# The second layer's modulation vectors made beside the first expert stage: a two-part network on one core

## The chip, the cores and the metric

The kernel runs on one core of a Trainium2 chip. The metric is the device time of one execution, in microseconds (us); lower is better. The core's engines are TensorE (PE, with its weight loads as PEld), VectorE (DVE), ScalarE (ACT), GpSimd (POOL) and SyncE (SP, which here only issues transfers). Each engine runs its own list of instructions in a fixed order and waits on semaphores; a transfer is queued by the engine that issues it.

## The reference, cut to what matters

Two networks of two layers each run one after the other on 1024 tokens of width 1024. The first is an S5 layer and an attention layer. The second has an even layer (window attention, a gating unit) and an odd layer (latent attention, a short convolution), each followed by a stage of 16 experts in which every expert takes the 128 tokens that it scores highest. The even layer also updates 256 context tokens, the odd layer does not.

Every layer is modulated: from one conditioning vector `c` come vectors that scale, shift and gate its activations.

```
silu_c, silu_cc = silu(c), silu(c_ctx)
for layer in range(2):
    m_lat = split(silu_c  @ mod_w[layer] + mod_b[layer], 6)      # six vectors of 1024
    m_ctx = split(silu_cc @ mod_w[layer] + mod_b[layer], 6)
    h = rms_norm(x, g1) * (1 + m_lat[1]) + m_lat[0]
    x = x + m_lat[2] * mixer(h)                                  # even or odd
    h = rms_norm(x, g2) * (1 + m_lat[4]) + m_lat[3]
    x = x + m_lat[5] * experts(h)
    ... the same for the context, in the even layer alone
return rms_norm(x, final_g)
```

The weights `mod_w[layer]` are 1024 by 6144 numbers of fp32. The vectors depend on `c` and weights only, so they may be made at any time before their use.

## The kernel before, in words

All products are fp32, made of three fp32r products each: a matrix is split into a high and a low part (`whi` on ACT, `wlo` on DVE, L282 and L283 for the expert weights, L241 and L242 for others), and `mm3` issues the three matmuls (L247 to L249).

**The modulation.** `mod_steps` makes one of the vectors ("a part", 1024 numbers) in eight steps of 128 columns. A step does the product of the weights with `silu(c)` on POOL, not on TensorE: in two halves, SP loads 512 by 128 weights (`mraw`, 256 KB, L364, two buffers), POOL multiplies them by the vector (L367), adds the halves of the result (L373), and gathers what is left into `macc` (L378 in the first half, L375 and L376 in the second). What remains is a sum over the 128 partitions, which PE does as a matmul of `macc` with a column of ones (L396, called "the sum" below); DVE adds the bias (L399) into a column or into `mrow`. After the eighth step `mrow` is transposed on PE and stored.

A step's sum isn't issued in the step itself but at the start of the next one, by `rest()`; a ninth entry of the list issues the last. Where the result goes in PSUM is `mod_psum`'s choice: one bank of its own (`pC`), or, while `self.attending` is set, one of three banks (`pT`) that the transposes use.

**When a step runs.** The list `self.behind` holds the steps of all parts in the order of their use, each with a weight (2 where the context's vector is made too, else 1). The loops of the layers call `tick()` after each group of products; a tick takes from the list as much weight as `self.rate[1]` says. `require(key)` runs at once all that is left up to a part that is about to be needed. So modulation runs beside the layers, from the S5 layer on. During the expert stages (`ffn`) the rate is (0, 0), so that none runs there. When the first expert stage begins, some 30 steps of weight 1 are still in the list (the rest of the second layer's first gate, then its scale, shift and gate around the experts); they run beside the odd layer.

**Who sets the order.** The code is traced once and a list scheduler, driven by a simulated timeline, puts the instructions of each engine in order: an instruction stands where its operands are ready in that timeline and its turn in the program has come. The chip then keeps to that order.

**The expert stage.** Per expert, POOL gathers 128 tokens (`xs`, L2253, one buffer), PE transposes them (L2202), and three products with 1024 by 1024 weights follow: w1 (`first`), w3 (`second`), w2 (`third`). SP loads the weights as 24 tiles of 512 KB (`exp_w`, L2172) into a ring of some 21 buffers; each is split by ACT and DVE into one of five buffers. After the 48 matmuls of a product, 16 short ones (L2241, into `pC`) do the context's tokens with the unsplit tiles, and only then is a tile's buffer free. POOL adds the results to memory (`x_d`, L2298, `c_d`, L2302).

After the 16th expert the odd layer begins: its weights (`wraw`, from `od_w_in`) and the tokens (`xin`, from `x_d`) are loaded by SP, the tokens are normalised (ACT L291, DVE L224, POOL `rstd` L226, DVE L305), transposed (PE L312) and modulated (L313, L314).

Of the kernel before, what the change touches and what calls it, by code (L numbers as in the profile page):

```python
# [9 lines left out]
F32 = mybir.dt.float32  # L10
# [10 lines left out]
P = 128  # L21
# [101 lines left out]
class Net:  # L123
# [223 lines left out]
    def mod_steps(self, W, vecs, part, use):  # L347


        nc = self.nc  # L350
        G = nc.gpsimd.tensor_tensor
        todo = []

        def rest():
            while todo:
                todo.pop(0)()

        def step(q):
            rest()
            c0 = part * D + q * P  # L360
            acc = self.mp.tile([P, 2, P], F32, name="macc", bufs=3)
            for h in range(2):
                raw = self.mp.tile([P, 4, P], F32, name="mraw", bufs=2)
                nc.sync.dma_start(raw, W[h * 512:(h + 1) * 512, c0:c0 + P].rearrange("(k p) c -> p k c", p=P))  # L364
                for i, v in enumerate(vecs):
                    t = self.mp.tile([P, 4, P], F32, name="mprod")
                    mul = G(t, raw, v[:, 4 * h:4 * h + 4, None].to_broadcast([P, 4, P]), OP.mult)  # L367
                    if self.hold is not None:

                        self.tc.add_manual_dep(mul.ins, self.hold.ins.name, mybir.DependencyInfo(  # L370
                            mybir.DependencyClass.Sync, mybir.DependencyReason.DATA), reason="hold")
                        self.hold = None
                    G(t[:, 0:2], t[:, 0:2], t[:, 2:4], OP.add)  # L373
                    if h:
                        G(acc[:, i], acc[:, i], t[:, 0], OP.add)  # L375
                        G(acc[:, i], acc[:, i], t[:, 1], OP.add)  # L376
                    else:
                        G(acc[:, i], t[:, 0], t[:, 1], OP.add)  # L378
            todo.append(lambda: use(q, [[acc[:, i]] for i in range(len(vecs))], self.ones))

        return [lambda q=q: step(q) for q in range(KT)] + [rest]

    def mod_psum(self):
# [1719 lines left out]
    def ffn(self, layer, m, x_d, c_d, out=None):  # L2103
# [4 lines left out]
        with ExitStack() as ctx:  # L2108
# [87 lines left out]
            def matT(rows, xt):  # L2196

                for b in range(2):
                    ps = self.psT.tile([P, 512], F32, name="pT")
                    for j in range(4):  # L2200
                        k = 4 * b + j
                        nc.tensor.transpose(ps[:, j * P:(j + 1) * P], rows[:, k * P:(k + 1) * P], self.id)  # L2202
                    sl = slice(4 * b, 4 * b + 4)
                    self.split(xt[0][:, sl].rearrange("p k s -> p (k s)"), xt[1][:, sl].rearrange("p k s -> p (k s)"), ps)

            def matTc(rows, xc):

                ps = self.psT.tile([P, 512], F32, name="pT")
                n = 2 * CCAP
                for k in range(4):  # L2210
                    nc.tensor.transpose(ps[:, k * n:(k + 1) * n], rows[:, k * P:(k + 1) * P], self.id[:n, :n])
                nc.scalar.activation(xc.rearrange("p (h k) s -> p k h s", h=2),
                                     ps[:, :4 * n].rearrange("p (k h s) -> p k h s", k=4, h=2), AF.Copy)
# [3 lines left out]
            def product(W, xt, xc, hook=None):  # L2217


                with ExitStack() as order:  # L2220
                    if chain:
                        order.enter_context(self.tc.issue_after(chain[-1]))
                    ps = self.psA.tile([P, 2, 512], F32, name="pA")
                    pc = self.psC.tile([P, 512], F32, name="pC") if xc is not None else None
                    raws = []
                    for k in range(KT):
                        raw, hi, lo = wtile(W, k)
                        raws.append(raw)
                        if hook is not None:
                            hook(k)  # L2230
                        for n in range(2):
                            c = slice(n * 512, (n + 1) * 512)
                            last = self.mm3(ps[:, n], xt[0][:, k], xt[1][:, k], hi[:, c], lo[:, c], k == 0, k == KT - 1)
                cs = None
                if xc is not None:

                    with self.tc.issue_after(last.ins):
                        for k in range(KT):
                            for n in range(2):
                                t = 32 * (2 * (k % 2) + n)  # L2240
                                last = nc.tensor.matmul(pc[t:t + 32], lhsT=xc[:, k], rhs=raws[k][:, n * 512:(n + 1) * 512],  # L2241
                                                        start=(k < 2), stop=(k >= KT - 2))
                    chain.append(last.ins)
                    cs = ep.tile([2 * CCAP, 512], F32, name="cs", bufs=2)
                    nc.scalar.activation(cs, pc[64:128], AF.Copy)
                    nc.vector.tensor_tensor(cs, pc[0:64], cs, OP.add)
                return ps.rearrange("p a b -> p (a b)"), cs
# [3 lines left out]
            def fetch(e):  # L2251
                xs = ep.tile([P, D], F32, name="xs", bufs=1)
                nc.gpsimd.indirect_dma_start(out=xs, out_offset=None, in_=h_d,  # L2253
                                             in_offset=bass.IndirectOffsetOnAxis(ap=idx[:, e:e + 1], axis=0))
                xts[e] = [ep.tile([P, KT, P], F32R, name=f"xt{i}", bufs=2) for i in range(2)]
                matT(xs, xts[e])
                xcs[e] = None
                if c_d is not None:
                    xsc = ep.tile([2 * CCAP, 512], F32, name="xsc", bufs=1)
                    nc.gpsimd.indirect_dma_start(out=xsc, out_offset=None, in_=half_rows(hc_d),  # L2260
                                                 in_offset=bass.IndirectOffsetOnAxis(ap=idxc[:, e:e + 1], axis=0))
                    xcs[e] = ep.tile([P, KT, CCAP], F32, name="xc", bufs=2)
                    matTc(xsc, xcs[e])

            def first(e):
                pa, ca = product(a["exp_w1_2"][layer, e], xts[e], xcs[e])
                gs[e] = ep.tile([P, D], F32, name="g", bufs=1)
                nc.scalar.activation(gs[e], pa, AF.Silu)
                if ca is not None:
                    cgs[e] = ep.tile([2 * CCAP, 512], F32, name="cg", bufs=1)  # L2270
                    nc.scalar.activation(cgs[e], ca, AF.Silu)

            def second(e):
                pb, cb = product(a["exp_w3_2"][layer, e], xts[e], xcs[e])
                nc.vector.tensor_tensor(gs[e], pb, gs[e], OP.mult)
                gts[e] = [ep.tile([P, KT, P], F32R, name=f"gt{i}", bufs=1) for i in range(2)]
                matT(gs[e], gts[e])
                gcs[e] = None
                if cb is not None:
                    nc.vector.tensor_tensor(cgs[e], cb, cgs[e], OP.mult)  # L2280
                    gcs[e] = ep.tile([P, KT, CCAP], F32, name="gc", bufs=1)
                    matTc(cgs[e], gcs[e])
# [42 lines left out]
                final_norm(r)  # L2325
                nc.sync.dma_start(out[t * P:(t + 1) * P], r)

            self.rate = (0, 0)

            fetch(0)  # L2330
            first(0)
            for e in range(NEXP):
                if e + 1 < NEXP:
                    fetch(e + 1)
                second(e)
                if e + 1 < NEXP:
                    first(e + 1)
                third(e)
                self.tick()

# [71 lines left out]
```

## Time and profile before

| | |
|---|---|
| time, median of 3 runs | 4264.09 us (4262.44 to 4264.76) |
| the profiled execution: time, span | 4259.37 us, 4257.6 us |
| PE busy | 3920.6 us, 92% of the span |
| DVE busy | 2777.5 us, 65% |
| ACT busy | 1972.0 us, 46% |
| POOL busy | 1552.8 us, 36% |
| mean granted clock of PE | 0.962 of full speed |
| modulation multiplies on POOL (L367) | 416, of 1.13 us in the mean |

The stages by time in the span: S5 tables until about 340 us, the S5 layer and the attention's projections until about 1090, attention and the even layer until about 2060, the first expert stage to 2836, the odd layer to about 3640, the second expert stage to the end. Busy shares are means over stages with different limits, so the views of single stretches decide.

### The profile page before, as it was taken

The numbers are of one execution on the slowest core, as the hardware profiler recorded it, in microseconds if no ns is written. First come the engines' busy times: TensorE is split into PE (matmuls) and PEld (weight loads), VectorE is DVE, ScalarE is ACT, GpSimd is POOL, SyncE is SP. The second block draws the span as 40 slices with busy tenths as digits, with TensorE's granted clock in tenths as the row PEclk, the third lists the DMA queues.
The fourth block names the chain that finished last, engine by engine and source line by source line (L and its number), as shares of the span: only waits on it lengthen the run. The fifth ranks groups of instructions, "written<-read, shape, count | busy, mean of one in ns | idle before, by whom it ended". The sixth has DMA issues, their size and how long they took to land.

```text
span 4257.6 us, 58517 instructions
## 1 busy us (share of the span) xinstructions
PE 3920.6 (92%) x21173; PEld 2974.9 (70%) x21173; DVE 2777.5 (65%) x3962; ACT 1972.0 (46%) x3029; POOL 1552.8 (36%) x1723
## 2 busy tenths in 40 slices
PE   7888889999999999999799999979989999799997
PEld 6777667777566888568466666658876667588775
DVE  8695555352556635664777777764546654899887
ACT  4323232321554312542466666652245542577775
POOL 1005889998646788002211111126800002111003
PEclk9999999999999999999799999989999999899999
DMA  7536565345663553234688787862451025899996
GB/s 239 167 138 216 184 206 176 128 134 181 152 142 99 191 150 123 72 131 163 230 292 294 285 291 282 284 223 87 125 158 34 26 99 211 298 387 382 373 374 249
DMA packets 512339, 848.91 MB, mean 199 GB/s; under 512 B 68061, under 2 KB 300626, under 8 KB 511474
## 3 DMA queue, kind: packets, MB, share of 16 engines
q1 hardware_dynamic: 498946, 802.16, 55.1%
q0 software_dynamic: 13104, 43.01, 4.1%
q8 instruction: 167, 2.74, 0.3%
q14 instruction: 122, 1.00, 0.1%
HBM read 714.82 MB, written 130.21 MB: 198 GB/s over the span
## 4 chain that ended last, share of the span: by engine, by line
PE 63%; POOL 13%; DVE 11%; DMA 6%; issue 4%; ACT 2%; SPq 1%; POOLq 0%; ACTq 0%; DVEq 0%
PE pA L247 14%; PE pA L248 14%; PE pA L249 14%; POOL mprod L367 5%; PE pC L1059 4%; PE pC L2241 4%; PE pT L1075 4%; POOL mprod L373 4%; DVE S L968 2%; DVE sc L967 2%; DVE wlo L283 2%; POOL macc L376 1%; POOL macc L378 1%; POOL macc L375 1%; PE pT L2202 1%
## 5 line engine op out<-in xcount | busy, mean ns | idle before, releaser
L283 DVE TENSOR_TENSOR wlo<-fraw,whi 128x1024 fp32r<-128x1024 f32 x650 | 788.9, 1239 | 128.7 <-ACT whi L282 122.0
L282 ACT ACTIVATE whi<-fraw 128x1024 fp32r<-128x1024 f32 x650 | 679.9, 1060 | 195.8 <-PE pA L249 182.2
L247 PE MATMUL pA<-whi,ah 128*128 128x512 f32 (+3 forms) x1584 | 592.6, 375 | 6.1 <-ACT ah L282 4.1
L248 PE MATMUL pA<-wlo,ah 128*128 128x512 f32 (+3 forms) x1584 | 591.4, 373 | 3.1 <-DVE wlo L242 3.1
L249 PE MATMUL pA<-whi,al 128*128 128x512 f32 (+3 forms) x1584 | 589.5, 372 | 0.0
L248 PE MATMUL pA<-wlo,xt 128*128 128x512 f32 x1024 | 411.6, 402 | 4.3 <-POOL wlo L2182 2.1
L247 PE MATMUL pA<-whi,xt 128*128 128x512 f32 x1024 | 409.9, 401 | 1.8 <-ACT xt L282 1.8
L249 PE MATMUL pA<-whi,xt 128*128 128x512 f32 x1024 | 406.0, 397 | 0.6 <-DVE xt L283 0.6
L367 POOL TENSOR_TENSOR mprod<-mraw,sil 128x512 f32<-128x512 f32 x320 | 362.4, 1132 | 95.1 <-DMA mraw<-mod_w 71.8
L373 POOL TENSOR_TENSOR mprod<-mprod 128x256 f32<-128x256 f32 x416 | 349.5, 840 | 31.2
L2253 POOL DMA_INDIRECT xs<-h_d,ixl x32 | 38.7, 1210 | 834.3 <-PE pT L2202 809.6
L247 PEld LDWEIGHTS pA<-whi,ah 128*128 128x128 f32 x1584 | 302.5, 191 | 54.3 <-ACT ah L282 4.2
L248 PEld LDWEIGHTS pA<-wlo,ah 128*128 128x128 f32 x1584 | 302.2, 191 | 52.1 <-DVE wlo L242 4.9
L249 PEld LDWEIGHTS pA<-whi,al 128*128 128x128 f32 x1584 | 301.9, 191 | 48.3 <-issue 1.2
L241 ACT ACTIVATE whi<-wraw 128x1024 fp32r<-128x1024 f32 (+3 forms) x130 | 131.0, 1017 | 409.8 <-PE pA L249 185.8
L1028 DVE TENSOR_REDUCE st<-pA 128x1 f32<-128x640 f32 (+4 forms) x208 | 200.5, 967 | 137.8 <-PE pA L1348 62.7
L242 DVE TENSOR_TENSOR wlo<-wraw,whi 128x1024 fp32r<-128x1024 f32 (+3 forms) x130 | 174.0, 1356 | 123.4 <-ACT whi L241 121.7
L249 PE MATMUL pA<-ah,wlo 128*128 128x512 f32 x576 | 230.8, 403 | 12.9 <-DVE wlo L242 12.9
L247 PEld LDWEIGHTS pA<-whi,xt 128*128 128x128 f32 x1024 | 193.0, 188 | 61.8 <-issue 13.4
L247 PE MATMUL pA<-ah,whi 128*128 128x512 f32 x576 | 230.9, 404 | 3.6 <-ACT ah L282 2.4
L248 PE MATMUL pA<-al,whi 128*128 128x512 f32 x576 | 231.9, 403 | 1.0 <-DVE al L283 0.9
L248 PEld LDWEIGHTS pA<-wlo,xt 128*128 128x128 f32 x1024 | 193.2, 189 | 52.9 <-DVE wlo L283 7.8
(569 smaller groups left out, 8279.0 us busy)
## 6 DMA issues: line engine op xcount, KB each, us to landing
fraw<-exp_w SPq DMA_DIRECT2D x665, 512.0 KB
wraw<-exp_w SPq DMA_DIRECT2D x99, 512.0 KB
mraw<-mod_w SPq DMA_DIRECT2D x192, 256.0 KB
mraw<-b_mod_w SPq DMA_DIRECT2D x48, 256.0 KB
wraw<-a_w_in SPq DMA_DIRECT2D x16, 512.0 KB
mraw<-kv_mod_w SPq DMA_DIRECT2D x32, 256.0 KB
wraw<-kv_w SPq DMA_DIRECT2D x16, 512.0 KB
kf_d<-hs SPq DMA_DIRECT2D x32, 256.0 KB
```

The costliest lines, as they stand in the source:

```text
L242: nc.vector.tensor_tensor(lo[:, :kk, :n], raw[:, :kk, :n], hi[:, :kk, :n].bitcast(F32), OP.subtract)
L247: mm(ps, lhsT=lh, rhs=rh, start=first, stop=False)
L248: mm(ps, lhsT=lh, rhs=rl, start=False, stop=False)
L249: return mm(ps, lhsT=ll, rhs=rh, start=False, stop=last)
L282: self.nc.scalar.activation(hi, src, AF.Copy)
L283: self.nc.vector.tensor_tensor(lo, src, hi.bitcast(F32), OP.subtract)
L367: mul = G(t, raw, v[:, 4 * h:4 * h + 4, None].to_broadcast([P, 4, P]), OP.mult)
L373: G(t[:, 0:2], t[:, 0:2], t[:, 2:4], OP.add)
L1028: nc.vector.tensor_reduce(st[:, i:i + 1], s, AX.X, OP.max, negate=True)
L1059: mm = nc.tensor.matmul(box["acc"][s * 64:(s + 1) * 64, c], lhsT=v(kt, s), rhs=pt[s][:, c], start=(kt == 0), stop=(kt == last))
L1075: nc.tensor.transpose(pt[:, j * P:(j + 1) * P], ps_[s][j](kt), self.id)
L2241: last = nc.tensor.matmul(pc[t:t + 32], lhsT=xc[:, k], rhs=raws[k][:, n * 512:(n + 1) * 512], start=(k < 2), stop=(k >= KT - 2))
```

## The change

Two things are changed. In `mod_steps`, a step's sum is issued two steps later than before (`rest(2)` leaves two in the list), and `macc` has four buffers for three. In `ffn`, the rate during the expert loop is (0, 3) for (0, 0), `attending` is set, so that sums there go to the banks `pT`, and each expert ticks twice: after `second` and, as before, after `third`. For the second expert stage the list is empty.

```diff
-        def rest():
-            while todo:
+        def rest(keep=0):
+            while len(todo) > keep:
                 todo.pop(0)()
 
         def step(q):
-            rest()
+
+            rest(2)
             c0 = part * D + q * P
-            acc = self.mp.tile([P, 2, P], F32, name="macc", bufs=3)
+            acc = self.mp.tile([P, 2, P], F32, name="macc", bufs=4)
...
-            self.rate = (0, 0)
+
+            self.rate, self.attending = (0, 3), True
 
             fetch(0)
             first(0)
...
                 second(e)
+                self.tick()
                 if e + 1 < NEXP:
                     first(e + 1)
                 third(e)
                 self.tick()
+            self.attending = False
```

What the scheduler makes of it is seen in the engines' orders. In the changed kernel most lines are one higher than before (L365 for L364, L397 for L396), and two higher in places.

SP's queue at the end of the first expert stage, before; `fraw` and `wraw` with `exp_w_2` are expert tiles, `wraw` with `od_w_in` the odd layer's first weights, `xin` its tokens, `mraw` the modulation's loads:

```order
L2172 DMA fraw<-exp_w_2 128x1024 x6
L238 DMA wraw<-od_w_in 128x2x512 x7
L364 DMA mraw<-mod_w 128x4x128
L238 DMA wraw<-od_w_in 128x2x512
L322 DMA xin<-x_d 128x2x1024 x4
L364 DMA mraw<-mod_w 128x4x128 x2
L322 DMA xin<-c_d 128x2x1024
L364 DMA mraw<-mod_w 128x4x128 x14
```

The same place now:

```order
L2173 DMA fraw<-exp_w_2 128x1024 x6
L238 DMA wraw<-od_w_in 128x2x512 x8
L322 DMA xin<-x_d 128x2x1024 x4
L322 DMA xin<-c_d 128x2x1024
L238 DMA wraw<-od_w_in 128x2x512 x4
L238 DMA wraw<-od_w_in 128x2x288 x4
```

No load of the modulation is left there; all of them have moved ahead, between the expert tiles. SP's queue within the first expert stage now, where it had only expert tiles:

```order
L2173 DMA fraw<-exp_w_2 128x1024 x6
L365 DMA mraw<-mod_w 128x4x128 x2
L2173 DMA fraw<-exp_w_2 128x1024 x7
L2173 DMA wraw<-exp_w_2 128x1024
L365 DMA mraw<-mod_w 128x4x128 x2
L2173 DMA wraw<-exp_w_2 128x1024 x2
L2173 DMA fraw<-exp_w_2 128x1024 x2
L365 DMA mraw<-mod_w 128x4x128
```

About nine of them stand among the 24 tiles of an expert, in the first seven experts. On PE, in the first expert stage now, sums stand between the matmuls of a product (`xt` is the expert's tokens); before there were none:

```order
L247 MATMUL pA<-whi,xt_19365 128x512
L397 MATMUL pT<-ones,macc 128x1
L248 MATMUL pA<-wlo,xt_19365 128x512
L397 MATMUL pT<-ones,macc 128x1
L249 MATMUL pA<-whi,xt_19366 128x512
```

On PE at about 968 us (the attention's projections), before; `hkn` are heads to be transposed:

```order
L1192 MATMUL pT<-cst,hkn 128x128 x8
L396 MATMUL pC<-ones,macc 128x1
L247 MATMUL pA<-ah_7223,whi 128x512
L248 MATMUL pA<-al_7224,whi 128x512
L249 MATMUL pA<-ah_7223,wlo 128x512
L247 MATMUL pA<-ah_7223,whi 128x512
```

And now:

```order
L1193 MATMUL pT<-cst,hkn 128x128 x8
L397 MATMUL pC<-ones,macc 128x1
L249 MATMUL pA<-ah_7213,wlo 128x512
L247 MATMUL pA<-ah_7213,whi 128x512
L248 MATMUL pA<-al_7214,whi 128x512
L249 MATMUL pA<-ah_7213,wlo 128x512
```

Counted through the list, this is the 79th sum in both orders: it stands where it stood. Of the 208 sums, the first 32 stand at their old places, the next sixty up to about 100 matmuls later and some not later at all, those beside the attention mostly 70 to 195 matmuls later.

## Rows read from the trace of the kernel before

**Rows 1.** Busy time by stretch: us, then each engine's busy us (instructions), clock, DMA share.

```profile
core 0: us, PE busy (x) PEld busy (x) DVE busy (x) ACT busy (x) POOL busy (x), PEclk, DMA share, GB/s
560.00:968.00 408.00, 377.75 (x1745) 296.50 (x1743) 222.78 (x279) 128.92 (x186) 378.54 (x407) 0.98 0.49 157
2060.00:2830.00 770.00, 767.27 (x4175) 508.27 (x4175) 593.83 (x556) 500.56 (x558) 86.30 (x59) 0.99 0.78 274
2830.00:2900.00 70.00, 45.75 (x223) 34.44 (x222) 43.78 (x67) 37.16 (x62) 49.41 (x55) 0.73 0.58 186
2900.00:3100.00 200.00, 195.73 (x1047) 173.09 (x1046) 89.44 (x166) 48.21 (x103) 135.53 (x170) 0.99 0.37 111
```

**Rows 2.** Chain that ended last, 2830 to 2876 us: start, duration, what.

```profile
2835.47 8.61 DMA wraw<-od_w_in
...
2845.26 1.82 DVE wlo L242
...
2847.64 5.76 DMA xin<-x_d
...
2855.78 0.18 DVE rs_v L224
...
2862.69 1.31 issue
...
2866.26 0.94 DVE rs_v L224
```

**Rows 3.** Timeline of PE, 2834 to 2874 us: start, duration, [idle before it, releaser].

```profile
2870.60 0.59 PE L396 MATMUL pC<-ones,macc 128*128 128x1 f32 x2 [1.20 <-POOL macc L376]
...
2872.11 1.20 PE L247 MATMUL pA<-ah,whi 128*128 128x512 f32 x2
```

**Rows 4.** Timeline of PE in the odd layer, 3028 to 3036 us.

```profile
3031.73 0.35 PE L396 MATMUL pC<-ones,macc 128*128 128x1 f32 x2 [2.66 <-DVE mrow L399]
3032.87 0.80 PE L1845 MATMUL pT<-cst,lrow 128*128 128x128 f32 x4 [0.79 <-ACT lrow L1840]
```

**Rows 5.** Timeline of PE around 968 us.

```profile
965.42 0.40 PE L249 MATMUL pA<-ah,wlo 128*128 128x512 f32 x1
965.65 0.40 PE L247 MATMUL pA<-ah,whi 128*128 128x512 f32 x1
968.64 0.38 PE L396 MATMUL pC<-ones,macc 128*128 128x1 f32 x2 [2.59 <-POOL macc L376]
...
971.48 0.63 PE L248 MATMUL pA<-al,whi 128*128 128x512 f32 x1
971.91 0.63 PE L249 MATMUL pA<-ah,wlo 128*128 128x512 f32 x1
```

**Rows 6.** PE's waits, 560 to 1090 us: total, times, longest.

```profile
PE pC L396 <- POOL macc L376: 25.4, 18, 2.6
```

**Rows 7.** POOL's groups, 2836 to 3100 us: count, busy us, mean ns, idle before.

```profile
L367 POOL TENSOR_TENSOR mprod<-mraw,sil 128x512 f32<-128x512 f32 x59 | 69.1, 1172 | 4.9 <-DMA mraw<-mod_w 0.6
L373 POOL TENSOR_TENSOR mprod<-mprod 128x256 f32<-128x256 f32 x59 | 49.2, 834 | 4.2
L378 POOL TENSOR_TENSOR macc<-mprod 128x128 f32<-128x128 f32 x30 | 18.8, 628 | 43.9 <-PE pC L396 42.2
```

**Rows 8.** DVE's splits of 128x1024 weights, first 340 to 740, then 2060 to 2830 us.

```profile
L242 DVE TENSOR_TENSOR wlo<-wraw,whi 128x1024 fp32r<-128x1024 f32 x29 | 44.9, 1559 | 34.6 <-ACT whi L241 34.3 <-PE pA L249 0.2
...
L283 DVE TENSOR_TENSOR wlo<-fraw,whi 128x1024 fp32r<-128x1024 f32 x326 | 399.3, 1225 | 109.6 <-ACT whi L282 105.4 <-DMA wraw<-exp_w 0.3 <-DMA fraw<-exp_w 0.3
```

**Rows 9.** Chain that ended last, 450 to 560 us.

```profile
515.59 8.76 DMA mraw<-kv_mod_w
...
542.00 5.36 DMA mraw<-kv_mod_w
```

**Rows 10.** Waits in the first expert stage, 2060 to 2830 us.

```profile
POOL xs L2253 <- PE pT L2202: 488.1, 14, 37.9
...
ACT whi L282 <- PE pA L249: 139.7, 302, 3.3
```

## The prediction

> **What bounds the kernel now.** I read the busy time by stretch first, then in each stretch that the change touches the chain of work that ended last, then PE's own timeline and waits.
>
> The first expert stage belongs to PE: it is busy 767.27 of 770 us [rows 1], and the waits listed there are those of other engines, among them POOL's 488.1 us behind PE before its gathers [rows 10]. One expert takes 767.27 / 16 = 48.0 us. POOL has 86.30 us of work in this stretch, 5.4 us per expert, so it is the emptiest engine of the kernel's fullest stage. The modulation's work is taken from 2836 to 3100 us, where POOL is busy 49.41 of 70 and 135.53 of 200 us, and PE lacks 24.3 us in the first of these stretches and 4.3 us in the second [rows 1]. Those 28.6 us are all that the move can win there. Earlier, from 560 to 968 us, POOL is busy 378.54 of 408 us and PE 377.75 [rows 1]: both are near full, and PE waits 25.4 us, 18 times until 1090 us, for a `macc` that POOL has not finished [rows 6].
>
> **The change part by part.** *What moves.* 59 multiplies with 59 halve-adds and 90 smaller adds leave the odd layer: 69.1 + 49.2 us, and three adds in each of 30 steps at 18.8 us per 30, 56.4 us, together 174.7 us of POOL [rows 7]. Their sums on PE and their loads go with them; these are moved, not added, and cancel.
>
> *The gain at the change of stage.* The chain from the last expert to the odd layer's first product goes through the loads of its weights (8.61 us), the last of their splits, then the load of the tokens (5.76 us) [rows 2], and only after that through work that POOL disturbs. The two loads stay, since they wait for buffers and for the experts' last result, not for the modulation; of the 24.3 us most is therefore out of reach. What I take away: the split of 1.82 us at 1.225 us, its price beside an idle POOL [rows 2, 8], 0.6 us; a break of 1.31 us inside a scaling of `xin` while a multiply runs, 1.3 us; `rs_v` in 0.94 instead of 0.18 us, 0.8 us [rows 2]; and a sum that holds the transposes up by 1.20 us right ahead of the first product at 2872.11 us [rows 3]. That is 3.9 us. SP's queue no longer holds loads of the modulation ahead of the tokens, and less traffic shares the DMA; for this I add 1.1 us, a fifth of the 5.76 us. Together **5 us**. Bounds: 2 us, if the split and the sum alone come back; 9 us, the 3.9 us and 5.1 of the 5.76 us, if the tokens' load were issued that much sooner.
>
> *The gain in the odd layer.* At 3031.73 us PE waits 2.66 us for the modulation and then 0.79 us for a row that was late with it [rows 4]. After a wait of this length PE runs slowly: behind the 2.59 us at 968.64 us its matmuls start 0.43 us apart where they were 0.23 us apart before, still so 3.3 us later [rows 5], so half of 3.3 us, 1.6 us, goes on top of a wait of over 2 us or so. 2.66 + 0.79 + 1.6 = **5 us**, bounds 3 (the row of 0.79 us and the clock stay, since another operand was late too) and 5.
>
> *The sums taken two steps later, and the fourth buffer.* If all the waits of [rows 6] went and nothing took their place, this would win 25.4 us and the slow matmuls behind the longer ones. I take **1 us**. POOL is as full as PE there [rows 1], its order is left nearly as it was, and PE needs more of it than the sums: the root for the heads' norms stands in the same queue behind the multiplies. A sum taken later lets PE go on until it meets POOL at the next place. And the scheduler doesn't move them all: the sum at 968.64 us, the longest wait of [rows 6], stands at its old place, so its 2.59 us stay. Bounds: 0 and 15 (the waits of under 2 us gone, with some slow matmuls).
>
> *The price in the expert stage, POOL and DVE.* 9 multiplies per expert with their adds cost POOL 9 x 174.7 / 59 = 26.6 us; with its 5.4 us it is busy 32 of 48.0 us. DVE has 593.83 / 16 = 37.1 us per expert [rows 1]. Beside a POOL that is busy nearly all the time, the split of a weight tile takes 1.559 us instead of 1.225 [rows 8]. At full overlap 24 tiles cost 24 x 0.334 = 8.0 us more, at two thirds of it 5.4 us: DVE goes to 42.5 of 48.0 us. It stays below PE, and five buffers of split tiles lie between them, so I cost it at nothing; without that cover it would be the 5.4 us in each of 6.6 experts. By the Trainium skill, "SBUF — State Buffer", section "Who interferes with whom", a DVE instruction with two inputs in SBUF and a GpSimd instruction that reads SBUF can't read together, and the one that comes second waits for the whole of the other; by that the sum would lose what the third rival below says, whereas the 0.334 us of the row would be part of one POOL instruction's length.
>
> *The price in the expert stage, the sums.* A sum now stands between two matmuls of PE's order. If its `macc` is late, everything behind it waits, and everybody waits for PE. What is late would be the loads: about 9 of 33 loads of an expert are the modulation's, so 48.0 / 9 = 5.3 us go from one multiply to the next, and two buffers give 10.7 us for a load and its multiply. A load of this kind took 5.36 us at best and 8.76 us beside other traffic [rows 9]; with the multiply's 1.17 us that is 6.5 to 9.9 us. It fits, with little to spare, and SP now holds expert tiles behind a load that waits for its buffer (they are issued early enough: ACT waits for PE here, not for tiles [rows 10]). The sums' two steps of delay help once and not for long, since POOL does 4.5 steps per expert and the ticks put 6 into the program. I expect four of some thirty sums late, at the 25.4 / 18 = 1.4 us of [rows 6], **6 us**. Bounds: 0, and 22 us, which is the 18 in 530 us of [rows 6] over the 320 us in question (11 waits, 15 us) with slow matmuls of 1.6 us behind four of them.
>
> *Sum.* 5 + 5 + 1 - 6 = 5 us less. The profiled execution took 4259.37 us, 4.7 us under the median of the runs, 4264.09, against which the new time is measured; 4259 less 5 for the median too: **4259 us**, 0.12% down. No difference under 0.2%, 8.5 us, can be told from none by measurements of this kernel.
>
> **The rivals.** (1) *The whole gain.* The sums in the expert stage are all in time and a part of the 25.4 us comes back: 5 + 5 + 5 to 12 us, 4242 to 4249 us. For it: ACT and DVE wait for PE throughout the stage, and the waits of [rows 6] average only 1.4 us, less than 25 matmuls at 0.23 us. Against it: POOL's 93% before 968 us. (2) *PE waits for `macc` in the expert stage,* the opposite sign. It decides as soon as a load and its multiply take over 10.7 us: each microsecond above costs half a microsecond per multiply, 30 us for 59, as far as the loads stand last in a burst of tiles. Loads of 11 to 12 us give 10 to 35 us of waits, less the 11 us won: 4266 to 4288 us. For it: the DMA share of 0.78 in this stage against 0.58 where a load of twice the size took 8.61 us [rows 1, 2]. Against it: a load of the modulation is half an expert tile. (3) *DVE and POOL exclude each other.* If the split never ran beside a multiply, 24 x 1.225 + 26.6 = 56 us would have to fit in 48.0: 8 us per expert, 53 us in 6.6 experts, 4264 - 11 + 53 = 4306 us. This is what the rule of the Trainium skill would do. Against it: from 560 to 968 us POOL's 378.54 and DVE's 222.78 us exceed the 408 us by far [rows 1]. (4) *Nothing moves:* the change of stage is held by the loads alone, and the wait at 3031 us turns into one for the late row: 2 us won, as much lost, 4264 us.
>
> **How the numbers follow.** The forecast, a few microseconds won in sum, has 0.40: by the bounds of its terms it lies between 4249 and 4264, and of the 0.40 some 0.12 are won by over 8.5 us. Rival 1 has 0.27, all of it faster. Rival 2 has 0.21, of which 0.05 lie within the bound. Rival 3 has 0.04, rival 4 0.08. Faster: 0.12 + 0.27 = 0.39; same: 0.28 + 0.05 + 0.08 = 0.41; slower: 0.16 + 0.04 = 0.20. The range leaves out rival 3, the upper part of rival 2 and the last of rival 1: 4244 to 4279 us; the forecast's own is 4249 to 4264.
>
> **What the changed profile would show.** Right: POOL at two thirds in the first seven experts and PE still without waits over 2 us there, splits of about 1.45 us on DVE, first product of the odd layer some 5 us earlier after the last expert, no wait at the place of 3031 us, and the waits for `macc` until 1090 us fewer but about as long in sum. Wrong: waits of PE for `macc` of 10 us and more in the expert stage (rival 2), for `wlo` (rival 3), or PE's 25.4 us before 1090 us down to a third (rival 1).

## The result and the profile after

The changed kernel is slower: 4293.29 us in the median of 7 runs (4277.59 to 4300.7) against 4263.98 us for the kernel before (4261.44 to 4266.52, 7 runs), a ratio of 1.007 with a 95% interval of 1.0058 to 1.0083. The forecast was 4259 us, with a range of 4244 to 4279. The profiled execution took 4300.7 us, with a span of 4298.9 us, the longest of its runs, 41.3 us over the span of the kernel before; the medians differ by 29.3 us only, so the profile shows more of the loss than a usual run has.

Where the 41 us lie is read from the times of four marks on PE's timeline in both traces:

| stretch | before, us | after, us | difference |
|---|---|---|---|
| start to the transposes of the first expert's tokens | 2056.4 | 2067.7 | +11.3 |
| from there to the end of the last expert's last matmul | 779.6 | 821.9 | +42.3 |
| from there to the odd layer's first product | 36.1 | 34.3 | -1.8 |
| from there to the transposes of `lrow` (3032.87 in [rows 4]) | 160.8 | 152.2 | -8.6 |
| the rest, to PE's last matmul | 1204.0 | 1202.1 | -1.9 |

The first row holds chance too: in the profiles of the runs below this mark moves between 2050.9 and 2066.7 us, and kernels that are equal up to it (before, and those with the old sums) show 2056.4 to 2065.1. The second row is the loss. Busy time by stretch of the changed kernel, first the third, then the sixth expert's stretch, then one in which the modulation is done:

```profile
core 0: us, PE busy (x) PEld busy (x) DVE busy (x) ACT busy (x) POOL busy (x), PEclk, DMA share, GB/s
2190.00:2245.00 55.00, 51.16 (x283) 34.46 (x279) 46.66 (x46) 31.41 (x36) 50.97 (x43) 0.97 0.94 318
2350.00:2415.00 65.00, 54.99 (x281) 36.42 (x277) 45.22 (x43) 31.38 (x35) 53.58 (x49) 0.89 0.80 267
2472.00:2521.00 49.00, 49.00 (x275) 32.65 (x273) 38.47 (x37) 32.29 (x37) 5.22 (x5) 1.00 0.83 282
```

By POOL's scatters to `x_d`, an expert took 48.3 us before; with the modulation beside it, it takes 48.4 to 62.0 us. In the first two of these stretches PE, which had next to no idle time in this stage [rows 1], has 3.8 and 10.0 us of it, its granted clock is 0.97 and 0.89, and POOL, which was to be busy two thirds of the time, is busy 93% and 82%. As soon as POOL is done with the modulation, PE is full again. PE's waits from 2080 to 2890 us, then POOL's groups from 2090 to 2520 us (count, busy us, mean ns, idle before):

```profile
PE pT L397 <- POOL macc L377: 18.7, 6, 4.6
PE pT L423 <- DVE mrow L400: 2.1, 1, 2.1
```

```profile
L368 POOL TENSOR_TENSOR mprod<-mraw,sil 128x512 f32<-128x512 f32 x61 | 86.9, 1425 | 24.6 <-DMA mraw<-mod_w 20.8
L374 POOL TENSOR_TENSOR mprod<-mprod 128x256 f32<-128x256 f32 x61 | 80.3, 1317 | 4.2
L379 POOL TENSOR_TENSOR macc<-mprod 128x128 f32<-128x128 f32 x31 | 30.2, 975 | 30.1 <-PE pT L397 28.1
L377 POOL TENSOR_TENSOR macc<-macc,mprod 128x128 f32<-128x128 f32 x31 | 29.8, 963 | 2.3
L376 POOL TENSOR_TENSOR macc<-macc,mprod 128x128 f32<-128x128 f32 x31 | 25.5, 824 | 2.2
```

The same instructions took 1172, 834 and 628 ns in the odd layer [rows 7]. A multiply with its share of the adds costs 252.7 / 61 = 4.14 us here, not 174.7 / 59 = 2.96 us. The chain that ended last shows what this does to PE (start, duration, what), in the sixth expert:

```profile
2373.95 14.21 DMA mraw<-mod_w
2388.29 1.05 POOL mprod L368
2389.41 1.59 POOL mprod L374
...
2400.65 1.91 POOL mprod L368
2402.63 0.73 POOL mprod L374
2403.43 0.45 POOL macc L376
2403.96 0.46 POOL macc L377
2404.47 0.59 PE pT L397 x2
2405.05 0.64 PE pA L248
2405.69 0.43 PE pA L249
...
2410.73 0.24 PE pA L249
```

The chain leaves PE, runs through a late load and then from one POOL instruction to the next, and comes back at the sum. Behind it PE's matmuls start 0.43 us apart, and 0.24 us apart again only some 6 us later. In this chain a multiply is 1.05 us long in some places and 1.91 in others, a halve-add 0.73 or 1.59.

From the start-to-start times of all of PE's records between the second expert's token transposes and the last expert's end, the 42.3 us divide so: waits 20.8 more; slower steps behind waits, 8.0 us in the three-pass products (557.2 against 549.2) and 7.0 in the context's matmuls (177.9 against 170.9); the sums and the transposes of `mrow` themselves 8.5; the other transposes 2.1 less.

The odd layer has its gain. PE's timeline at the change of stage, which answers to [rows 3]:

```profile
2910.06 3.87 PE L312 MATMUL pT<-cst,xin 128*128 128x128 f32 x16 [20.47 <-DVE xin L305]
2914.82 1.11 PE L312 MATMUL pT<-cst,xin 128*128 128x128 f32 x4 [0.89 <-ACT htmp L314]
2917.87 1.11 PE L312 MATMUL pT<-cst,xin 128*128 128x128 f32 x4 [1.93 <-ACT htmp L314]
2921.07 1.11 PE L312 MATMUL pT<-cst,xin 128*128 128x128 f32 x4 [2.08 <-ACT htmp L314]
2923.08 1.12 PE L312 MATMUL pT<-cst,xin 128*128 128x128 f32 x4 [0.90 <-ACT htmp L314]
2923.85 1.20 PE L247 MATMUL pA<-ah,whi 128*128 128x512 f32 x2
```

The sums are gone from here, and PE waits first in one piece, for the tokens, and then between the transposes for ACT's `htmp`. Ahead of the stage, the waits from 740 to 968 us in the changed kernel:

```profile
PE pA L247 <- DVE rs_v L224: 7.5, 1, 7.5
PE pA L247 <- DVE hkn L1149: 3.5, 2, 2.5
PE pC L397 <- POOL macc L377: 2.5, 3, 1.2
```

In the kernel before the wait for `macc` was 12.8 us in this stretch, and there was none for `rs_v`. The sums' waits have become waits for the heads' norms, whose roots stand in POOL's queue: behind the longest, DVE's `rs_v` was done at 748.92 us, and POOL came to its root (`rstd`, L226) at 756.37 us, after two multiplies and four adds that began since.

### The profile page after: what moved, and what is told of

Its sections match the earlier page's. It is cut to its first block, busy times and chain, and to the rows that moved or that the text cites. A ratio compares the mean times of both kernels' runs of the same rounds, so it can differ in the third digit from the quotient of the medians.

```text
span 4298.9 us, 58521 instructions
## 1 busy us (share of the span) xinstructions
PE 3936.8 (92%) x21173; PEld 2992.5 (70%) x21173; DVE 2779.6 (65%) x3962; ACT 1969.9 (46%) x3029; POOL 1630.4 (38%) x1723
## 4 chain that ended last, share of the span: by engine, by line
PE 58%; POOL 17%; DVE 10%; DMA 7%; issue 5%; ACT 2%; SPq 1%; POOLq 0%; DVEq 0%; ACTq 0%
PE pA L247 12%; PE pA L248 12%; PE pA L249 12%; POOL mprod L368 6%; POOL mprod L374 4%; PE pC L1060 4%; PE pT L1076 4%; PE pC L2242 3%; DVE S L969 2%; POOL macc L379 2%; DVE sc L968 2%; POOL macc L377 2%; POOL macc L376 1%; DVE wlo L283 1%; DMA fraw<-exp_w 1%
## 5 line engine op out<-in xcount | busy, mean ns | idle before, releaser
L283 DVE TENSOR_TENSOR wlo<-fraw,whi 128x1024 fp32r<-128x1024 f32 x650 | 819.5, 1291 | 114.3 <-ACT whi L282 108.7
L368 POOL TENSOR_TENSOR mprod<-mraw,sil 128x512 f32<-128x512 f32 x320 | 376.5, 1176 | 95.7 <-DMA mraw<-mod_w 72.9
L374 POOL TENSOR_TENSOR mprod<-mprod 128x256 f32<-128x256 f32 x416 | 377.0, 906 | 30.7
L226 POOL TENSOR_TENSOR rstd<-rs_v,mhalf 128x2 f32<-128x2 f32 (+3 forms) x62 | 85.2, 1376 | 513.6 <-DVE rs_v L224 513.5
```

The costliest lines, as they stand in the source:

```text
L283: self.nc.vector.tensor_tensor(lo, src, hi.bitcast(F32), OP.subtract)
```

## The experiments

Theory 1 says that PE loses its time in the expert stage at sums whose `macc` is late, because POOL is slower there than PE's order has it. Its rivals: half of the loss comes from the later sums ahead of the stage (theory 2), or the loads and the contention of POOL and VectorE slow the experts themselves. Ratios are to runs of the kernel before on the same chip, with 95% intervals.

**The two parts apart.** First the expert stage's part alone, with `rest()` and three buffers as before:

```diff
-            rest(2)
+            rest()
-            acc = self.mp.tile([P, 2, P], F32, name="macc", bufs=4)
+            acc = self.mp.tile([P, 2, P], F32, name="macc", bufs=3)
```

> The steps run in the first expert stage as in the change, but a step's sum is issued with the next step and macc has three buffers, as before. Theory 1 (POOL, slowed by DVE beside it, can't keep the pace that PE's order gives it, so PE stands at the sums): the stage from the first gather's transposes to the last expert loses at least the 42 us of the changed kernel, 42 to 65 us, PE waits for macc 20 us and more in it, the odd layer gains 12 us, total 4290 to 4315 us. Theory 2 (half of the loss comes from the sums taken later, in the stretches ahead of the stage): the first gather's transposes stand at 2056 us as before, and the total is 7 to 11 us below the changed kernel with the same loss in the stage.

Measured: ratio 1.0043 (1.0029 to 1.0058), 18 us slower. The stage from the second expert's transposes loses 32.3 us in the profile (795.5 against 763.2), with

```profile
PE pT L397 <- POOL macc L377: 17.5, 8, 4.9
```

and the odd layer and what follows gain 16.0 us. Both theories missed: theory 1 had 42 us and more for the stage, waits of 20 us and more, and a total from 4290 us up, where the median is 4279.18 us; theory 2 had the total about right (by the two ratios 0.0027 x 4260 = 11.5 us below the changed kernel), but not the same loss in the stage. What stays of theory 1 is that the stage alone loses, at sums whose `macc` is late.

Then the later sums alone:

```diff
-            self.rate, self.attending = (0, 3), True
+            self.rate = (0, 0)
...
                 second(e)
-                self.tick()
...
-            self.attending = False
```

> The sums are issued two steps later and macc has four buffers, but no step runs in the first expert stage. Theory 1: the stage stays at 780 us, the total is that of before within 4 us (4260 to 4268). Theory 2: 4 to 11 us are lost ahead of the stage, total 4268 to 4275 us, with waits of PE for the heads' norms (DVE rs_v, hkn) between 740 and 968 us in place of those for macc.

Measured: ratio 1.0015 (1.0003 to 1.0027), 6 us slower. The stage is as before (780.3 us). From 740 to 968 us the wait for `macc` is 4.0 us and

```profile
PE pA L247 <- DVE rs_v L224: 8.1, 1, 8.1
```

stands in its place. So the later sums are a small loss of their own, and both theories have a part: 18 us from the stage and 6 from the sums. The 5 us that are left of the 30 lie within the three intervals, of 5 to 6 us to either side each; whether the two parts add to each other isn't shown.

**A pace that wasn't one.** Two runs were meant to halve the pace with the rate (0, 1):

> The changed kernel with the rate (0, 1) in the expert stage: two steps per expert over fifteen experts instead of 4.5 over seven. Theory 1: POOL needs some 17 us per expert and is on time, PE waits under 3 us for macc in the stage, the stage costs only the sums' own 8 us and a few us of low clock, the odd layer still gains 12 us: 4255 to 4268 us, by whether the 11 us ahead of the stage are real. Rival (the loads of the modulation or DVE's slower splits delay the experts whatever the pace): the stage still loses 20 us and more, total above 4270 us.

> As the run with one step a tick, but the sums issued with the next step and three buffers for macc. Theory 1: at two steps per expert the sums' delay isn't needed, total 4254 to 4264 us, the same as with the later sums or below it by what those lose ahead of the stage. Rival: without the delay PE waits for macc at each of the thirty sums, 1.4 us each, 40 us more than with it.

They didn't do that. When the stage begins the list's first entry has weight 2, the last sum of a part with two vectors, and a tick of rate 1 never takes it; no step ran in the stage, whose length was 779.8 and 780.0 us. So they say nothing of a pace, and repeat other kernels: the first the later sums alone, at 1.0014 (1.0003 to 1.0026), the second the kernel before, at 1.0 (0.9988 to 1.0012). The first shows the loss of 6 us again, the second is a control.

**The sums much later.** The stage's part at its full pace, with the sums far behind their steps:

```diff
+            while len(self.todo) > 11:
+                self.todo.pop(0)()
...
+                acc = self.accp.tile([P, 1, P], F32, name="macc1", bufs=13)
...
-            nraw = 18 if c_d is not None else 21
+            nraw = 17 if c_d is not None else 21
```

> The changed kernel with the sums of the expert stage issued eleven steps later instead of two, across the parts, into thirteen small buffers of their own (the ring of expert tiles gives one of its buffers up for them); POOL's work and the loads in the stage stay. Theory 1 (PE loses time at sums whose macc is late): PE waits under 3 us for macc in the stage, which loses 8 to 14 us (the sums' own time, some low clock) in place of 42; total 25 to 34 us under the changed kernel. Rival (the loads and POOL's and VectorE's contention delay the experts themselves): the stage still loses over 20 us, with PE waiting for wlo, for tiles or for the gathers.

Measured: ratio 1.0014 (1.0 to 1.0028) against the changed kernel's 1.007, which is 0.0056 x 4260 = 24 us less, about what theory 1 had. PE has no wait for `macc` in the stage, and busy time from 2090 to 2480 us reads

```profile
2090.00:2480.00 390.00, 390.00 (x2171) 260.86 (x2169) 351.83 (x314) 251.71 (x282) 315.05 (x235) 1.00 0.92 324
```

PE 100%, DVE 90%, POOL 81%, the clock full. From the second expert's transposes the stage loses 3.1 us (766.3 against 763.2), under theory 1's 8 to 14, and far from the rival's 20. The last eleven sums stand behind the last expert here. POOL's instructions were no faster (multiplies of 1.56 us, halve-adds of 1.45), and the DMA share is 0.92, so neither delays the experts. It is the wait at the sum that costs, with the slow matmuls behind it.

**Why POOL is slow.** The changed kernel without VectorE's part of the split in the first expert stage (the high part stands in for the low one there):

```diff
+                elif layer == 0:
+                    nc.scalar.activation(hi, raw, AF.Copy)
+                    lo = hi
                 else:
                     self.split(hi, lo, raw)
```

> The changed kernel, in which the first expert stage leaves out VectorE's part of the weights' split (the high part stands in for the low one), so that VectorE has 8 us of work per expert in place of 37. If VectorE beside it is what makes POOL late: the halve-adds fall from 1.33 to under 0.9 us, the multiplies from 1.41 to under 1.15 us, PE waits under 8 us for macc in the stage, which loses under 18 us. If late loads make POOL late: the same times per instruction, but PE still waits 15 us and more, and POOL 20 us and more for mraw.

POOL's groups in it, 2080 to 2500 us, and the waits of its multiplies and of PE's sums:

```profile
L368 POOL TENSOR_TENSOR mprod<-mraw,sil 128x512 f32<-128x512 f32 x61 | 65.2, 1070 | 100.9 <-DMA mraw<-mod_w 98.4
L374 POOL TENSOR_TENSOR mprod<-mprod 128x256 f32<-128x256 f32 x61 | 50.1, 821 | 4.0
L376 POOL TENSOR_TENSOR macc<-macc,mprod 128x128 f32<-128x128 f32 x31 | 15.4, 498 | 2.3
```

```profile
PE pT L397 <- POOL macc L377: 2.1, 1, 2.1
```

All of POOL's instructions are below their means in the odd layer [rows 7], PE waits 2.1 us in place of 18.7, and the ratio is 1.0004 (0.9994 to 1.0015). POOL now waits 98.4 us for loads, 26 times, and this doesn't reach PE. So VectorE's splits beside POOL make it late, not the loads.

The trace of the changed kernel shows how. First POOL's timeline, then DVE's, at 2313 us:

```profile
2312.67 1.04 POOL L368 TENSOR_TENSOR mprod<-mraw,sil 128x512 f32<-128x512 f32 x1
2313.79 1.60 POOL L374 TENSOR_TENSOR mprod<-mprod 128x256 f32<-128x256 f32 x1
```

```profile
2312.71 2.08 DVE L283 TENSOR_TENSOR wlo<-fraw,whi 128x1024 fp32r<-128x1024 f32 x1 [0.44 <-ACT whi L282]
```

The split begins 0.04 us behind the multiply and ends 1.08 us after it (2314.79 against 2313.71 us); the halve-add begins within the split and ends 0.60 us after it. So it goes throughout, by the start and end times of the records: from 2090 to 2520 us 120 of POOL's 215 multiplies and adds begin while a split runs, and 119 of them end after the split; the 40 halve-adds among them end at least 0.58 us after it and take 1.55 us in the mean, against 0.84 for the 14 that have no split beside them. The other way round, 108 splits that begin while POOL multiplies or adds take 1.56 us in the mean, 55 with none of these beside them 1.22. By these times the two kinds of instruction hardly do their work at the same time: whichever begins second ends only well after the other.

**A slower pace.** Without the added tick, first with the later sums, then with the sums as before:

```diff
                 second(e)
-                self.tick()
                 if e + 1 < NEXP:
```

> The changed kernel without the added tick: some 2.7 steps per expert over eleven experts in place of 4.5 over seven. Theory 1: POOL, busy about 28 of 48 us, is on time, PE waits under 5 us for macc in the stage, which loses 8 to 16 us; the odd layer gains 12 us; with the 6 us that the later sums cost ahead of the stage the total is that of before within 8 us, 4256 to 4270. Rival (each load among the expert tiles costs, whatever the pace): the stage loses as much as in the changed kernel, 35 us and more.

> The same without the added tick, with the sums issued with the next step and three buffers as before. Theory 1: no loss ahead of the stage, 8 to 20 us lost in the stage (a sum has less slack), 12 to 16 us won in the odd layer: 4253 to 4268 us, at or under the kernel before. Rival (the delay is what keeps the sums from stopping PE in the stage): PE waits 15 us and more for macc in the stage, total 4275 us and more.

Measured: 0.9993 (0.9981 to 1.0005) and **0.9971 (0.996 to 0.9983)**: 4256.28 and 4247.3 us against 4259.84. The second is 12 us faster than the kernel before, and differs from the first experiment's kernel, which is 18 us slower, in the pace alone. In neither does PE wait for `macc` in the stage. In the faster one, from 2090 to 2640 us,

```profile
2090.00:2640.00 550.00, 550.00 (x3069) 368.97 (x3068) 457.25 (x442) 356.78 (x399) 306.48 (x241) 1.00 0.89 314
```

with POOL at 56%, though its halve-adds take 1.41 us; and POOL waits for PE now, not PE for POOL:

```profile
POOL macc L379 <- PE pT L397: 141.5, 9, 23.6
```

The stage from the second transposes takes 764.2 us, 1.0 more than before, where theory 1 had put 8 to 20, and what follows it 11.6 less; so the total lies below theory 1's 4253 too. The rival, that the delay is what keeps the sums from stopping PE, falls: at this pace no delay is needed.

**Which half of the later sums' part costs.** The faster kernel with the fourth buffer alone, and the full pace with the sums eleven steps later in the stage only:

> The run with one tick and the sums issued with the next step (12 us under the kernel before), with the fourth buffer of macc added. If the loss of 5 to 9 us that the later sums showed in three pairs of runs is the sums' delay: no more than 3 us above that run, ratio to before 0.996 to 0.998. If it is the fourth buffer, which lets POOL run further ahead of the heads' norms: the loss appears here, ratio 0.998 to 1.0005.

> The full pace of the change (two ticks, rate 3), the sums eleven steps later inside the expert stage alone; ahead of it the sums and the three buffers are those of before. Theory 1: the pace itself costs nothing when PE is kept off the late sums: no waits for macc in the stage, the stage loses 2 to 5 us, the odd layer gains 12 to 15 us, ratio to before 0.996 to 0.9985. Rival (POOL at 80% and DVE's splits cost the stage more than that at the full pace): ratio 0.9985 and above, as in the run with eleven steps and the later sums everywhere, 1.0014.

Measured: 0.9982 (0.9972 to 0.9992) and 0.9995 (0.9982 to 1.0008). The first lies between the kernels with and without the later sums (0.9993 and 0.9971), and its interval meets both: which half of that part costs the 5 to 9 us stays open. The second has no wait for `macc` in the stage and a sum of gains and losses near nothing; its interval holds the boundary of the two expectations. Theory 1's ratio for it was too good, so the full pace still costs some microseconds more than the slow one, of which its one profile shows 2.9 us of PE's waits for the gathers in the stage and 5.9 us for `mrow` behind the last expert, where the last eleven sums stand.

## Why the prediction was wrong, step by step

**The change of stage, 5 us.** Mis-sized: 1.8 us. The tokens were asked for 10.6 instead of 11.6 us after the last expert, which is 1.0. From there to the first product the time is 23.7 us instead of 24.5, which is 0.8, where I had taken 3.3 for the break, `rs_v` and the sum. The wait of 1.20 us at the sum went, but PE's waits between the transposes are 5.8 us in total after 5.9 before: they came back at `htmp`.

**The odd layer, 5 us.** Right, and too small: the stretch to `lrow` lost 8.6 us, the wait of [rows 4] went, and with it, it seems, the slow matmuls behind it and the sums' own time, which I had let cancel; how the 8.6 divide wasn't measured. Both gains together, 10 us, came out at 10.4.

**The later sums, 1 us.** Wrong in sign by little. The reason given was right: POOL is as full as PE there and the waits come back at the next place, the heads' norms. In the traces the waits of PE of over 0.15 us from 340 to 1090 us sum to 74.6 us before and 73.7 after, 55.0 and 41.0 of them at sums. The loss of 6 us, in the runs, isn't explained by these waits, nor do the profiles show where it lies: the first mark of the table stands at 2060.4 us in the mean of five kernels with the old sums and at 2061.2 us in six with the later ones.

**"Moved, not added, and cancel".** This failed for the sums, in part. In the changed kernel's expert stage, where PE has no idle time, they take 8.5 us of it with the transposes of `mrow`, and the other transposes 2.1 less. But they needn't cost that: in the run with one tick and the old sums they take 6.2 us there, PE's other work takes 5.3 less, and the stage is 1.0 us longer.

**The price in the expert stage, POOL and DVE.** The step that failed first. (Its sum has a small slip: the three adds of a step took 54.1 us in 30 steps, not three times the 18.8 of one of them, 56.4.) I took POOL's 26.6 us per expert from the odd layer's rows, where DVE is busy less than half of the time [rows 1], and asked only what POOL does to DVE, not what DVE does to POOL. At 4.14 us per multiply, nine are 37 us in place of 26.6, and POOL with its gathers is busy 93% and 82% in the stretches above, where I had two thirds. For DVE the estimate held: its splits grew to 1.493 us (the larger group, 124 tiles) against the 1.45 that I named, and PE didn't wait for them.

**The price in the expert stage, the sums, 6 us.** This term, 6 us, was the error in the total: the stage lost 42.3 us in the profile, 32.3 in that of the stage's part alone, both over my bound of 22. It rests on the step before it: POOL, slowed by DVE, brought `macc` late. The bound came from waits per microsecond in a stretch in which POOL's instructions were often at their short times, and it priced the low clock at four places of 1.6 us; measured, the waits are 20.8 us, the slow steps 15.0. The number of waits, 6 of them over 0.3 us, was near the four that I expected; they were 3.1 us long, not 1.4. Waits for `macc` of 18.7 us in the stage are what the prediction itself named as its sign of being wrong.

**The rivals and the range.** The time came out in rival 2's way, and above the 4266 to 4288 us that I gave it (by its own terms, 10 to 35 us of waits less 11, the lower end is 4263; and the 11 to 12 us are those of a load with its multiply). Loads were only a part of it: one did come late (14.21 us), and POOL waits 20.8 us for them in all, but the run without VectorE's splits waits longer for loads and loses nothing in the stage.

Rival 3, exclusion of DVE and POOL, to which I gave 0.04, has the mechanism that makes POOL late. What I held against it, busy times that add up to more than the stretch, decides nothing, since the time in which one instruction waits for the other counts as busy in both; so it is with the 351.83 and 315.05 us of the same 390 above. Its price was wrong: by the pieces that follow the other's end (1.08 us of a split, 0.90 of a multiply, 0.60 of a halve-add, 0.32 of a small add, medians of the trace, as an estimate) 24 splits and nine multiplies with their adds fill an estimated 43.7 us of an expert's 48.3, not 56, DVE's other work and POOL's gathers left out. So DVE kept its pace, and PE had no wait for `wlo` in the stage; what was lost is POOL's punctuality at the sums. By the Trainium skill ("SBUF — State Buffer", "Who interferes with whom") the order in which the two issue decides which of them blocks. The trace agrees, with halve-adds of 0.73 us or 1.59 and splits of 1.22 or 1.56. I had priced DVE's side of it alone.

The range was narrower than its own terms: their bounds add up to 4235 to 4281 us, not to the 4249 to 4264 that I gave the forecast. The measured 4293.29 us lies outside of both, since the one term of the sums exceeded its bound.

## What to carry to other kernels

Work that is put on an idle engine beside a full stage must be priced with the neighbours that it will have there, for both of them: POOL's halve-adds took 1.3 us in the stage with VectorE's splits and 0.8 us without them. If the bound engine has to pick up a result in its fixed order, what counts is not whether the helper's load fits on average but whether it is done at each pick-up; here, with the sums as before, one tick per expert (some 2.7 steps) cost the stage 1 us and won 12 us in all, two ticks (some 4.5 steps) lost 18. A wait of the bound engine is dearer than its length where its clock falls behind it: 15 us on top of 21.

## What the runs showed that I had not expected

A wait of PE in a stage where it had been full can halve its rate for some microseconds after, also with everything ready. Five of the six waits at the sums, of 2.09 to 4.61 us, were followed by matmuls that start 0.43 us apart instead of 0.23; the sixth, of 1.76 us, and the wait of 2.11 us at `mrow` were not. Behind the waits of 4.61 and 2.11 us:

```profile
2325.00:2331.00 6.00, 5.48 (x16) 3.77 (x20) 2.53 (x3) 1.43 (x2) 1.73 (x2) 0.52 0.70 256
2374.00:2380.00 6.00, 5.71 (x33) 4.53 (x34) 3.34 (x7) 3.55 (x6) 2.49 (x4) 1.00 1.00 380
```

The granted clock is 0.52 in the first, near the lower of PE's two levels (1.2 GHz), and 1.00, the upper one (2.4 GHz), in the second.
